# A list scheduler's rule for its filler work: the scalar engine's budget no longer gates it, and two groups of steps are placed elsewhere

## The chip, the cores and the metric

The kernel runs on one core of a Trainium2 chip. A core has a matrix engine (TensorE; PE in the profile, PEld for its weight loads), a vector engine (VectorE; DVE), a scalar engine (ScalarE; ACT), GpSimd (POOL) and a sync engine (SyncE; SP). In this kernel SP issues the weight loads and POOL issues the small reshuffling DMAs. Each engine works through its own instructions in order and waits at semaphores for the others. The metric is the device time of one execution in microseconds (us); less is better.

## The reference

The program computes two layers of an encoder trunk on 256 tokens of width 2048. Per layer, cut to what matters:

```python
h = rmsnorm(x, norm_g)
(c_a, c_glu, c_gate, q_down, kv_down, k_pe, m_gate, g_conv, g_mla) = split(h @ w_in)
# branch A
u = c_a * sigmoid(c_glu)
u = causal_depthwise_conv(u, conv_w, width=31) + conv_b
y_conv = (silu(layernorm(u)) * silu(c_gate)) @ w_proj_conv
# branch B: 16 heads, low-rank q and kv, rotary part of 64, block-causal mask in chunks of 64
q = rope(rmsnorm((rmsnorm(q_down) @ w_uq) per head))
k = rope(rmsnorm((rmsnorm(kv_down) @ w_ukv, k_pe) per head))
y_mla = (softmax(mask(q k^T * scale)) v * silu(m_gate)) @ w_proj_mla
# merge
x = x + (sigmoid(g_conv) * y_conv + sigmoid(g_mla) * y_mla) @ w_out
```

The rotary tables are sines and cosines of the positions times 32 inverse frequencies; they are computed once and serve both layers. The convolution is 31 taps per channel: a multiply-add over all tokens for each tap.

## The kernel before

**Products.** All matrix products run on TensorE in float32r. To keep float32 accuracy each operand is separated into a high and a low part, and a product takes three matmuls (high by high, high by low, low by high). The weights come from HBM in pieces of two 128-row blocks by up to 512 columns (`load`, five buffers, issued on SP). For each piece ScalarE makes the high part (`split_hi`, one cast) and VectorE the low part (`split_lo`, one subtraction). In the step of piece i the high part of piece i+3 and the low part of piece i+2 are issued (lines 181 and 281 to 285), and there are four and three buffers for them. So VectorE may lag behind TensorE's need by something under two steps before TensorE waits.

**Slots.** One piece is one slot: 12 matmuls on TensorE, then a call of `background(n)` (lines 242 to 260). A layer has 344 slots. `order_of_layer` gives the blocks: `glu` 0, `down` 0 to 2, `glu` 1 and 2, then eight rounds (one for each pair of heads) of `uq`, `ukv` and a further `glu` or `cgate` block, then the rest of `cgate`, `mgate`, `gmla`, `pmla`, `gconv`, `pconv` and `wout` blocks. `uq` and `ukv` blocks have two slots, all others eight.

**Two kinds of work beside the products.** Steps with a due slot are registered by `at_slot(ahead, f, vec, act)`. They run when their slot comes, and their stated costs are taken off a budget. The attention of a pair of heads is such a chain, placed by the constants of lines 67 and 68: squares and factors at 2 and 3 slots after the pair's `ukv` block, the turned queries and keys fetched at 7, transposed at 11, separated at 14 and 15 (with the subtractions a slot later), scores at 17, maxima at 18, exponentials at 19 with the probabilities written out by DMA, fetched back at 24, transposed at 29, values at 32.

The other kind has no due slot: `fill`, one queue in strict order. It holds the convolution (`conv`, 31 taps for each of 8 channel blocks of 256, queued when a block's input has been turned) and, queued by `layernorm` after the last pair, everything between the convolution and the `pconv` product: the mean (a matmul), subtracting it (`centre`, 8), the variance (a matmul), the reciprocal root in four pieces, scaling (`apply`, 8, each followed by a SiLU on ScalarE a slot later), the gate (`turned_gate` and `gated`, 8 each), and the separation of the result into high and low parts. A task may name a mark (`after`) and a number of slots that must have passed since.

**The budget.** At each slot both engines get the slot's length less the cost of the weight separation:

```python
slot = 12 * (n / 2400 + 0.0133) - 0.04
for e, split_us in (("vec", KS * n / 960 + 0.06), ("act", KS * n / 1066 + 0.04)):
    budget[e] = min(budget[e], 0.0) + slot - split_us
```

A debt is carried on; what is left over is lost. After the due steps, tasks are taken from `fill` while both budgets are above zero. For n = 512 that is 2.68 - 1.13 = 1.55 us for VectorE and 2.68 - 1.00 = 1.68 us for ScalarE.

**A tap** (lines 830 to 858) takes one of two forms. On VectorE alone it is two fused multiply-adds (cost 0.81). If ScalarE has scaled the input for it beforehand (`scale`, two activations, cost 0.85 of ScalarE), it is one addition on VectorE (cost 0.62). A tap orders the scaling of the next one where more than 0.8 is left in ScalarE's budget.

**At `pconv`** the product needs the whole normalised and gated convolution. The loop `while "yc" not in keep: run_fill()` and `before_pconv` take whatever is still in `fill` then, without looking at budgets, and TensorE's matmuls behind it wait for the result.

**Rotary tables.** `rope_tables` is a generator of 11 stages: two small loads (inverse frequencies, positions) on SP, nothing, the angles, six stages of range reduction on VectorE, and two stages with the sine activations. In layer 0, at `down` block 1, the stages are placed in slots 0 to 10 from the block's beginning. The same region has, counted from the start of the kernel, the loads of the layer's constants in slot 10 (`load_consts`, two DMAs on SP), the row factors `sum_x` in slot 13 (VectorE), and the evacuation of `glu` block 0 in slot 14. Slots 9 to 16 are `down` 0, 17 to 24 are `down` 1, 25 to 32 are `down` 2.

Of the kernel before, what the change touches and what calls it, by code (L numbers as in the profile page):

```python
# [63 lines left out]
EVAC_AT = 1  # L64
FETCH_AT, TURNED_AT = 4, 8

STATS_AT, SCALE_AT, QK_BACK_AT, QK_TURN_AT, ROPE_AT, NOPE_AT, SCORES_AT = 2, 3, 7, 11, 14, 15, 17
MAX_AT, EXP_AT, P_BACK_AT, P_TURN_AT, P_SPLIT_AT, VALUES_AT, O_AT = 18, 19, 24, 29, 30, 32, 34

REVOLUTION_PIECES = 6  # L70

# [44 lines left out]
def trunk(ctx: ExitStack, tc: tile.TileContext, xT, x, g_in, pos, win, wuq, wukv, wpc, wpm, wo, cst, rows, invf, out):  # L116
# [19 lines left out]
    pe, vec, act, gps, sp = (InOrder(e) for e in (nc.tensor, nc.vector, nc.scalar, nc.gpsimd, nc.sync))  # L136
# [83 lines left out]
    steps, clock, late = [], [0], []  # L220
    fill, budget, marks, owed = deque(), {"vec": 0.0, "act": 0.0}, {}, []

    def at_slot(ahead, f, vec=0.0, act=0.0):
        steps.append((clock[0] + ahead, (vec, act), f))

    def spend(costs):
        budget["vec"] -= costs[0]
        budget["act"] -= costs[1]
# [10 lines left out]
    def mark(name):  # L239
        marks[name] = clock[0]  # L240

    def background(n):
        clock[0] += 1
# [3 lines that stand above are left out]
        while True:  # L247
            due = [e for e in steps if e[0] <= clock[0]]
            if not due:
                break  # L250
            steps[:] = [e for e in steps if e[0] > clock[0]]
            for _, costs, f in due:
                spend(costs)
                f()
        while fill and budget["vec"] > 0 and budget["act"] > 0:
            after, slots = fill[0][1]
            if after and clock[0] < marks.get(after, 1 << 30) + slots:
                break
            run_fill()
        finish_late()  # L260

    def finish_late():
        while late:
            late.pop(0)()

    def run_fill():

        f, (after, _) = fill.popleft()
        while owed and after and after not in marks:
            owed.pop(0)()  # L270
        spend(f() or (0.0, 0.0))
# [29 lines left out]
    def stat_of(hi, lo):  # L301
        return lambda k, t: (hi[:, k, t * P : (t + 1) * P], lo[:, k, t * P : (t + 1) * P])
# [14 lines left out]
    def fetched(d, n):  # L317
        z = wide_p.tile([P, 4, n // P, 32], F32, tag="w", name="turned")
        fetch(d, z.rearrange("p i c s -> p (i c s)"))
        return z  # L320
# [152 lines left out]
    for l in range(DEPTH):  # L473
# [343 lines left out]
        def conv(b, us=us, vs=vs, s1=s1, C=C):  # L817
            scaled = {}

            def weight(k, j):  # L820
                at = C_CW + (2 * b + j) * CONV_W + k
                return C[:, at : at + 1]

            def scale(k):

                scaled[k] = wide_p.tile([P, 2, SEQ], F32, tag="w", name="tap")
                for j in range(2):
                    act.activation(scaled[k][:, j, :], us[b][:, j, k : k + SEQ], AF.Copy, scale=weight(k, j))

            def tap(k):  # L830

                if k == 0:
                    vs[b] = uv_p.tile([P, 2, PAD + SEQ], F32, tag="uv", name="v_t")
                u, v, costs = us[b], vs[b], (0.81, 0.0)
                if k == 0:
                    for j in range(2):
                        bias = C[:, C_CB + 2 * b + j : C_CB + 2 * b + j + 1]
                        vec.tensor_scalar(v[:, j, :SEQ], u[:, j, :SEQ], weight(k, j), bias, op0=ALU.mult, op1=ALU.add)
                elif k in scaled:
                    vec.tensor_add(v[:, :, :SEQ], v[:, :, :SEQ], scaled.pop(k))  # L840
                    costs = (0.62, 0.0)
                else:
                    for j in range(2):
                        vec.scalar_tensor_tensor(
                            v[:, j, :SEQ], u[:, j, k : k + SEQ], weight(k, j), v[:, j, :SEQ], op0=ALU.mult, op1=ALU.add
                        )
                if budget["act"] > 0.8 and 0 < k < CONV_W - 1:
                    scale(k + 1)
                    costs = (costs[0], 0.85)
                if k == CONV_W - 1:  # L850
                    mark(("s1", b))
                    if b == 0:
                        vec.tensor_copy(s1, v[:, :, :SEQ])
                    else:
                        vec.tensor_add(s1, s1, v[:, :, :SEQ])
                    costs = (costs[0] + 0.6, costs[1])
                    us.pop(b)
                return costs

            for k in range(CONV_W):  # L860
                fill.append((lambda k=k: tap(k), (None, 0)))

        def layernorm(vs=vs, s1=s1, C=C, keep=keep):
            stats = work2.tile([P, 5, SEQ], F32, tag="qk", name="ln_stats")
# [64 lines left out]
            def ahead(c):  # L929
                gates[c] = [fetched(d, 512) for d in keep["parked"][c]]  # L930
# [3 lines left out]
                return 0.65, 0.0  # L934

            def then(f, *args, after=None, slots=0):
                fill.append((lambda: f(*args), (after, slots)))

            fill.insert(max(len(fill) - 6, 0), (lambda: ahead(0), (None, 0)))
            for t in range(T):  # L940
                then(turned_gate, 0, t)
            then(mean, after=("s1", 7), slots=1)
# [174 lines left out]
        for kind, i, pl in planned:  # L1117
            if kind == "glu":
                at = EVAC_AT
                if i == 0 and l == 0:  # L1120
                    at = 6
                    for n, (t, c) in enumerate([(0, 0), (0, 2), (1, 0), (1, 2)]):
                        begin, end = first_sums(t, c)
                        at_slot((4, 5, 6, 9)[n], begin)
                        at_slot((9, 9, 10, 12)[n], end, 0.0, 1.5)
                    at_slot(13, sum_x, 2.2)
                elif i == 0:
                    at_slot(5, sum_x, 2.2)
                if i == 0:
                    at_slot(10, load_consts)  # L1130
                product(pl, uses_h, lambda t, ps, i=i: glu_evac(i, t, ps), at, (0.9, 2.2))
            elif kind == "down":
                if l == 0 and i == 1:
                    tables = rope_tables()
                    for a in range(11):
                        at_slot(a, lambda: next(tables, None), 0.0 if a < 2 else 1.6)
                product(pl, uses_h, lambda t, ps, i=i: down_evac(i, t, ps), costs=(0.0, 1.0))
                if i == len(DOWN_BLOCKS) - 1:
                    down_after()
            elif kind == "uq":  # L1140
                if i == 0:
                    attention_tiles()
                product(pl, of_down(0), lambda t, ps, i=i: uq_evac(i, t, ps), costs=(0.0, 2.3))
                at_slot(EVAC_AT + 1, lambda i=i: rotate_q(i), 1.2)
            elif kind == "ukv":
                product(pl, of_down(4), lambda t, ps, i=i: ukv_evac(i, t, ps), costs=(0.75, 2.6))
                attention(i)
                if i == NPAIR - 1:
                    layernorm()
            elif kind == "mgate":  # L1150
                product(pl, uses_h, lambda t, ps, i=i: mgate_evac(i, t, ps), costs=(1.25, 1.4))
            elif kind == "gmla":
                product(pl, uses_h, lambda t, ps, i=i: gmla_evac(i, t, ps), costs=(0.0, 2.7))
            elif kind == "pmla":
                product(pl, stat_of(*keep["o"]), lambda t, ps, i=i: pmla_evac(i, t, ps), costs=(1.25, 0.0))
            elif kind == "gconv":
                product(pl, uses_h, lambda t, ps, i=i: gconv_evac(i, t, ps), costs=(0.0, 3.9))
            elif kind == "cgate":
                product(pl, uses_h, lambda t, ps, i=i: cgate_evac(i, t, ps), costs=(0.0, 2.0))
            elif kind == "pconv":  # L1160
                while "yc" not in keep:
                    run_fill()
                product(pl, stat_of(*keep["yc"]), lambda t, ps, i=i: pconv_evac(i, t, ps), costs=(2.4, 0.0),
                        before=before_pconv if i == 0 else None)
            else:
                wout_begin(i)
                last = last_layer and i == 3
                product(pl, stat_of(*keep["y"]), lambda t, ps, i=i, f=wout_evac: f(i, t, ps),
                        0 if last else EVAC_AT, (1.25, 1.5))
# [103 lines left out]
```

## Time and profile before

| what | us |
|---|---|
| median of 3 runs | 1962.25 |
| lowest and highest of them | 1960.39, 1964.64 |
| the profiled execution, its own time | 1963.85 |
| its span, first to last instruction | 1961.9 |
| TensorE busy in the span | 1912.8 |
| VectorE busy | 1598.0 |
| ScalarE busy | 1350.8 |
| GpSimd busy | 371.1 |

The profile is of one execution. A page gives the busy time of each engine, the busy share in 40 equal slices of the span, the costliest groups of instructions and the DMA issues. Further views list the waits (who waited for whom), the instructions in order of time, and the busy time of each engine in chosen stretches. A line of code there is that of a helper through which every instruction is issued (L127), so instructions are told apart by the names of their tiles: `lo<-raw,hi` is the low part of a weight piece, `hi<-raw` the high part, `tap<-u_t,cst` the scaling of a tap, `v_t<-v_t,tap` a tap's addition, `v_t<-u_t,cst,v_t` half of a tap on VectorE alone, `acc` a product's accumulator, `ycT` the separated operand of `pconv`, `s` the scores, `qk_t` their operands.

### The profile page before, as it was taken

To read this page: it belongs to the slowest core of one execution; us is meant where nothing else is said; L and a number is where in the kernel's file an instruction comes from. 1 tells how busy PE (TensorE), PEld (TensorE's weight loads), DVE (VectorE), ACT (ScalarE), POOL (GpSimd) and SP (SyncE) were. 2 spreads that over 40 slices of the span, in tenths; PEclk is the share of its full clock that TensorE was granted. 3 is DMA by queue.
4 is the path that set the end of the run, shared out by engine and by line. 5 is a ranking of instruction groups with operands and counts; after the bars stand their busy time and mean duration, and the time that the engine had idled before them with its cause. 6 is when DMAs were issued, how large, how long until landed. Compare 5 with 4: busy or idle time off the path is not lost. (4 is left out here: it accounts for less than half of the span.)

```text
span 1961.9 us, 27462 instructions
## 1 busy us (share of the span) xinstructions
PE 1912.8 (97%) x8787; PEld 1607.8 (82%) x8787; DVE 1598.0 (81%) x2592; ACT 1350.8 (69%) x2385; POOL 371.1 (19%) x694
## 2 busy tenths in 40 slices
PE   9999999999999999699999999999999999997999
PEld 8888888888888887488889888888888888885887
DVE  6888887889999998566669788878899999985654
ACT  6577878878787885444557678688778878764442
POOL 1023434332200000021210333343322000001200
PEclk9999999999999999799999999999999999998999
DMA  8657877777755556277866687777767655664764
GB/s 307 204 198 255 269 241 253 257 247 231 239 195 199 187 205 214 86 236 242 292 216 201 210 261 246 238 249 258 246 229 240 201 196 185 210 210 137 246 226 162
DMA packets 135569, 437.73 MB, mean 223 GB/s; under 512 B 22784, under 2 KB 26624, under 8 KB 135424
## 3 DMA queue, kind: packets, MB, share of 16 engines
q1 hardware_dynamic: 104688, 359.63, 54.4%
q0 software_dynamic: 30304, 76.06, 12.6%
q8 instruction: 69, 1.13, 0.2%
q14 instruction: 76, 0.62, 0.1%
q10 hardware_dynamic: 432, 0.28, 0.0%
HBM read 395.51 MB, written 40.37 MB: 222 GB/s over the span
## 5 line engine op out<-in xcount | busy, mean ns | idle before, releaser
L127 ACT CAST hi<-raw 128x1024 fp32r<-128x1024 f32 (+3 forms) x689 | 703.4, 1024 | 525.1 <-PE acc L127 441.3
L127 DVE TENSOR_TENSOR lo<-raw,hi 128x1024 fp32r<-128x1024 f32 (+3 forms) x689 | 811.9, 1183 | 247.5 <-PE acc L127 180.3
L127 PE MATMUL acc<-hi,hT 128*128 128x512 f32 (+2 forms) x1728 | 525.9, 383 | 0.0
L127 PEld LDWEIGHTS acc<-hi,hT 128*128 128x128 f32 x1728 | 322.7, 188 | 59.6
L127 PE MATMUL acc<-lo,h_hi 128*128 128x512 f32 (+2 forms) x864 | 331.1, 383 | 2.8 <-DVE lo L127 2.8
L127 PE MATMUL acc<-hi,h_hi 128*128 128x512 f32 (+2 forms) x864 | 331.3, 383 | 0.7 <-ACT hi L127 0.7
L127 PE MATMUL acc<-lo,hT 128*128 128x512 f32 (+2 forms) x864 | 330.7, 383 | 0.1
L127 PE MATMUL acc<-hi,h_lo 128*128 128x512 f32 (+2 forms) x864 | 330.2, 382 | 0.0
L127 ACT ACTIVATE tap<-u_t,cst 128x256 f32<-128x256 f32 x634 | 274.9, 499 | 0.0
L127 DVE TENSOR_TENSOR v_t<-v_t,tap 128x512 f32<-128x512 f32 x317 | 218.4, 689 | 21.2 <-ACT tap L127 4.7
L127 PE MATMUL acc<-hi,ycT 128*128 128x512 f32 x512 | 171.1, 415 | 31.7 <-ACT ycT L127 31.7
L127 PEld LDWEIGHTS acc<-lo,h_hi 128*128 128x128 f32 x864 | 162.2, 188 | 34.9 <-DVE lo L127 5.5
L127 PEld LDWEIGHTS acc<-hi,h_hi 128*128 128x128 f32 x864 | 162.4, 188 | 30.6 <-ACT hi L127 1.2
L127 PEld LDWEIGHTS acc<-lo,hT 128*128 128x128 f32 x864 | 162.5, 188 | 30.4 <-DVE lo L127 0.8
L127 PEld LDWEIGHTS acc<-hi,h_lo 128*128 128x128 f32 x864 | 162.2, 188 | 30.1
L127 POOL DMA_DIRECT2D turned<-turn_d x82 | 46.0, 561 | 596.9 <-DVE v_t L127 191.7
L127 PE MATMUL acc<-hi,yT 128*128 128x512 f32 x512 | 158.5, 389 | 0.0
L127 PE MATMUL acc<-hi,oT 128*128 128x512 f32 x512 | 157.9, 389 | 0.0
L127 POOL DMA_DIRECT2D turn_d<-gate x176 | 95.9, 552 | 301.9 <-DVE gate L127 253.1
L127 PEld LDWEIGHTS acc<-hi,ycT 128*128 128x128 f32 x512 | 103.5, 202 | 58.0 <-ACT ycT L127 34.7
L127 PE MATMUL acc<-hi,qkc 128*128 128x512 f32 (+1 forms) x512 | 146.9, 362 | 0.0
L127 DVE SCALAR_TENSOR_TENSOR v_t<-u_t,cst,v_t 128x256 f32<-128x256 f32 x326 | 140.9, 479 | 1.4
(165 smaller groups left out, 2259.3 us busy)
## 6 DMA issues: line engine op xcount, KB each, us to landing
raw<-in_win SPq DMA_DIRECT2D x383, 512.0 KB, 4.3
raw<-in_wpm SPq DMA_DIRECT2D x64, 512.0 KB, 3.3
raw<-in_wpc SPq DMA_DIRECT2D x64, 512.0 KB, 4.0
raw<-in_wo SPq DMA_DIRECT2D x64, 512.0 KB, 4.4
raw<-in_wukv SPq DMA_DIRECT2D x32, 512.0 KB, 4.0
turned<-turn_d POOLq DMA_DIRECT2D x50, 256.0 KB, 4.4
raw<-in_win SPq DMA_DIRECT2D x32, 384.0 KB, 4.3
raw<-in_wuq SPq DMA_DIRECT2D x32, 384.0 KB, 3.1
```

Of the source, the lines that this page charges most:

```text
L127: ins = getattr(self.engine, name)(*a, **k)
```

## The change

Three parts. The loop over `fill` looks at VectorE's budget alone; ScalarE's counts only for tasks that say so in a third entry, and `apply` is the one that does (it must not be negative then). Scores, maxima, exponentials and the fetch of the probabilities stand one slot later; what follows them stays. The rotary tables start at `down` block 0, two slots after its beginning, in place of the beginning of block 1, and their stated cost is 1.8 in place of 1.6.

```diff
-STATS_AT, SCALE_AT, QK_BACK_AT, QK_TURN_AT, ROPE_AT, NOPE_AT, SCORES_AT = 2, 3, 7, 11, 14, 15, 17
-MAX_AT, EXP_AT, P_BACK_AT, P_TURN_AT, P_SPLIT_AT, VALUES_AT, O_AT = 18, 19, 24, 29, 30, 32, 34
+STATS_AT, SCALE_AT, QK_BACK_AT, QK_TURN_AT, ROPE_AT, NOPE_AT, SCORES_AT = 2, 3, 7, 11, 14, 15, 18
+MAX_AT, EXP_AT, P_BACK_AT, P_TURN_AT, P_SPLIT_AT, VALUES_AT, O_AT = 19, 20, 25, 29, 30, 32, 34
...
-        while fill and budget["vec"] > 0 and budget["act"] > 0:
-            after, slots = fill[0][1]
-            if after and clock[0] < marks.get(after, 1 << 30) + slots:
+        while fill and budget["vec"] > 0:
+            after, slots, scalar = fill[0][1]
+            if after and clock[0] < marks.get(after, 1 << 30) + slots or scalar and budget["act"] < 0:
                 break
             run_fill()
...
-        f, (after, _) = fill.popleft()
+        f, (after, _, _) = fill.popleft()
...
-                fill.append((lambda k=k: tap(k), (None, 0)))
+                fill.append((lambda k=k: tap(k), (None, 0, False)))
...
-                fill.append((lambda: f(*args), (after, slots)))
-
-            fill.insert(max(len(fill) - 6, 0), (lambda: ahead(0), (None, 0)))
+                fill.append((lambda: f(*args), (after, slots, f is apply)))
+
+            fill.insert(max(len(fill) - 6, 0), (lambda: ahead(0), (None, 0, False)))
...
-                if l == 0 and i == 1:
+                if l == 0 and i == 0:
                     tables = rope_tables()
                     for a in range(11):
-                        at_slot(a, lambda: next(tables, None), 0.0 if a < 2 else 1.6)
+                        at_slot(a + 2, lambda: next(tables, None), 0.0 if a < 2 else 1.8)
```

## The prediction

> **What bounds the kernel now.** First the page: busy time by engine, and two rows of the 40 slices.
>
> ```profile
> PE 1912.8 (97%) x8787; PEld 1607.8 (82%) x8787; DVE 1598.0 (81%) x2592; ACT 1350.8 (69%) x2385; POOL 371.1 (19%) x694
> ...
> PE   9999999999999999699999999999999999997999
> ...
> PEclk9999999999999999799999999999999999998999
> ```
>
> TensorE is the bound except in two places: slice 17, where its busy share and its clock both drop, and slice 37. The waits of TensorE say what is late there:
>
> ```profile
> PE acc L127 <- ACT ycT L127: 31.7, 7, 5.6
> PE s L127 <- DVE qk_t L127: 6.8, 18, 1.9
> PE acc L127 <- DVE lo L127: 2.8, 7, 0.7
> ```
>
> (Total, times, longest, in us.) `ycT` is `pconv`'s operand: the convolution branch is not ready. What it costs shows in stretches: length, then busy time and count of PE, PEld, DVE, ACT, POOL, then the granted clock and the DMAs.
>
> ```profile
> 475.00:700.00 225.00, 225.00 (x1001) 186.52 (x1000) 216.97 (x302) 178.80 (x298) 16.46 (x30) 1.00 0.61 206
> 760.00:788.00 28.00, 22.86 (x101) 18.59 (x99) 23.34 (x36) 17.90 (x25) 2.19 (x4) 0.95 0.61 202
> 788.00:835.00 47.00, 31.97 (x96) 24.39 (x97) 23.02 (x35) 19.19 (x27) 0.00 (x0) 0.74 0.26 88
> 1764.00:1805.00 41.00, 29.44 (x98) 22.49 (x98) 21.78 (x32) 17.92 (x24) 0.00 (x0) 0.79 0.34 116
> ```
>
> Undisturbed, 1001 matmuls leave in 225 us (a few merely straddle an edge): 0.226 us each, so a slot of 12 is 2.72 us. `pconv` block 0 has 96 matmuls and so needs 21.8 us. In layer 0 the stretches of 28 and 47 us hold 197 matmuls, 44.5 us of work, and lose 30.5; in layer 1 41 us hold 98, 22.1 us, and lose 18.9. Together 49.4: the 31.7 of waiting, and 17.7 in which the granted clock is 0.74 to 0.95 behind the waits.
>
> By a rule of the Trainium skill ("TensorE: Matmul & The Clock Gate", Part 1) the array falls to half clock after an idle window of about 3.4 us and needs one busy window to come back; estimated from that page, seven stalls would add at most 7 x 1.7 = 12 us and both stalls would be worth 44. The granted clock agrees in kind; the trace's 17.7 us is more, and it decides.
>
> **Part 1: the filler without ScalarE's gate.** Is VectorE's time there to be had? Taking the loop slot by slot with the code's own costs, in layer 0 before `pconv` 53 slots end with VectorE budget left because ScalarE's is used up, 31.9 us lost in all (layer 1: 53 and 33.2); `fill` comes to `pconv` with 18 tasks in layer 0 and 11 in layer 1. The same count gives 317 assisted taps and 163 on VectorE alone, which is what the trace has:
>
> ```profile
> L127 DVE TENSOR_TENSOR v_t<-v_t,tap 128x512 f32<-128x512 f32 x317 | 218.4, 689 | 21.2 <-ACT tap L127 4.7 <-DVE v_t L127 0.5
> L127 DVE SCALAR_TENSOR_TENSOR v_t<-u_t,cst,v_t 128x256 f32<-128x256 f32 x326 | 140.9, 479 | 1.4
> L127 ACT ACTIVATE tap<-u_t,cst 128x256 f32<-128x256 f32 x634 | 274.9, 499 | 0.0
> ```
>
> (326 halves are 163 taps.) With the new condition the count gives 264 assisted and 216 alone: ScalarE sheds 53 x 2 x 0.499 = 53 us, VectorE is charged 53 x (0.81 - 0.62) = 10 us more, 5 per layer. Of layer 0's 31.9 us, 27 remain, 27 / 1.55 = 17 slots: the mean's matmul goes from slot 267 to slot 250. `fill` is then empty in slot 274, `pconv` begins in slot 281; in layer 1 it is empty nine slots ahead. The loop at `pconv` finds nothing to run. That removes the stall whole, waits and clock: **-49.4 us**.
>
> Does VectorE carry a budget that is used up in every slot? The durations say no: 1.2 us for a low part and 0.96 for a tap alone exceed the stated 1.13 and 0.81. But a duration is not what an instruction takes from its successor:
>
> ```profile
> 600.31 1.22 DVE L127 TENSOR_TENSOR lo<-raw,hi 128x1024 fp32r<-128x1024 f32 x1
> ...
> 601.45 0.88 DVE L127 SCALAR_TENSOR_TENSOR v_t<-u_t,cst,v_t 128x256 f32<-128x256 f32 x2
> ...
> 602.24 1.22 DVE L127 TENSOR_TENSOR lo<-raw,hi 128x1024 fp32r<-128x1024 f32 x1
> ...
> 603.38 1.49 DVE L127 TENSOR_TENSOR v_t<-v_t,tap 128x512 f32<-128x512 f32 x2
> 604.90 0.69 DVE L127 TENSOR_TENSOR s1c<-s1c,v_t 128x512 f32<-128x512 f32 x1
> 605.51 1.22 DVE L127 TENSOR_TENSOR lo<-raw,hi 128x1024 fp32r<-128x1024 f32 x1
> ```
>
> From start to start the low part takes 1.14, a tap alone 0.79, an addition 0.61 where the next instruction does not need it and 0.75 where it does. The stated costs are right on average. And some blocks are already filled to the last slot by this count, `gmla` 1 and `pmla` 1 of layer 0 among them:
>
> ```profile
> 541.50:563.30 21.80, 21.80 (x98) 18.03 (x97) 21.14 (x30) 18.25 (x29) 0.00 (x0) 1.00 0.50 172
> 628.60:650.30 21.70, 21.70 (x97) 17.99 (x96) 20.82 (x29) 18.25 (x33) 0.00 (x0) 1.00 0.56 191
> ```
>
> VectorE is busy 97% there and TensorE never waits. So a full budget is just carried; the matmuls are its cover. In the attention stretch TensorE's slots are longer than planned (scores and values are not in `slot`):
>
> ```profile
> 238.30:264.10 25.80, 25.45 (x125) 21.30 (x124) 22.86 (x54) 18.97 (x41) 6.75 (x13) 1.00 0.71 228
> 1214.50:1244.30 29.80, 27.60 (x125) 22.51 (x124) 25.64 (x55) 19.75 (x42) 8.57 (x16) 0.94 0.68 225
> ```
>
> 25.8 us for 8 slots, against 21.4 planned: there is more room. A full queue leaves less slack behind VectorE's own waits, though. Bounds: 0, and 1 us for each of the 16 pairs, 16 us; I take **+1**, near the saturated blocks, which show none.
>
> ScalarE's gate stays for `apply`: it costs waiting in at most 8 slots per layer by the count, inside the margin of 7 and 9 slots. If that margin were gone, each missing slot would cost 2.72 us.
>
> **Part 2: scores a slot later.** The subtractions that make the scores' operands are issued in slot 16 after the pair, the scores stood in 17; a VectorE that lags more than a slot makes TensorE wait there, with all further matmuls behind it. The two rows above are the same block with the same 125 matmuls: the second has the longest of these waits (1.9) and the clock at 0.94, and is 4.0 us longer; so 2 us of clock come on top of the 6.8 of waits. A slot later the operands have to be ready no later than the low part that TensorE needs next anyway. Bounds -3 (the large waits alone) and -9; I take **-7**. On VectorE the maxima follow in the next slot as before. POOL issues the fetch of the probabilities a slot later, four slots ahead of the transposition:
>
> ```profile
> L127 POOL DMA_DIRECT2D pr<-turn_d x16: 567/567/570, 202.6 to 1427.6; - x16
> L127 DVE STREAM_TRANSPOSE pr<-pr x16: 944/948/951, 218.4 to 1448.4; 128x768 f32<-128x768 f32 x16
> ...
> DMA to landing us min/median/max: 2.4/3.4/5.5
> ```
>
> Issued at 202.6, used at 218.4: 15.8 us for 5.5 at most; one slot less costs nothing. The four write-out DMAs per pair now stand behind, not ahead of, the next pair's fetch on POOL's queue (both were in slot 19), which can only help that fetch.
>
> **Part 3: the rotary tables.** They move from slots 17 to 26 to slots 10 to 20, six slots, not eight. What they cost now, against the same blocks in layer 1:
>
> ```profile
> 47.40:65.30 17.90, 17.48 (x99) 16.60 (x97) 12.68 (x44) 7.31 (x10) 3.22 (x7) 1.00 0.57 179
> 65.30:81.70 16.40, 14.81 (x97) 14.02 (x96) 13.28 (x37) 8.87 (x15) 0.00 (x0) 1.00 0.62 203
> 1027.60:1044.30 16.70, 16.70 (x99) 16.70 (x98) 15.51 (x27) 12.99 (x24) 0.00 (x0) 1.00 0.57 174
> 1044.30:1058.30 14.00, 14.00 (x97) 14.00 (x96) 13.58 (x24) 12.87 (x24) 0.00 (x0) 1.00 0.71 220
> ```
>
> 34.3 against 30.7: 3.6 us lost. The new place is worse. Its two loads go out in slot 10, right behind the constants on SP, and `sum_x` falls among the stages:
>
> ```profile
> 34.78 0.42 SPq L127 DMA_DIRECT2D down<-in_rows  x1
> ...
> 37.53 0.96 DVE L127 TENSOR_TENSOR lo<-raw,hi 128x768 fp32r<-128x768 f32 x1 [1.14 <-ACT hi L127]
> 39.18 0.96 DVE L127 TENSOR_TENSOR lo<-raw,hi 128x768 fp32r<-128x768 f32 x1 [0.69 <-PE acc L127]
> 40.05 0.15 DVE L127 TENSOR_REDUCE totx<-ss_x 128x2 f32<-128x8 f32 x1
> ...
> 42.53 0.96 DVE L127 TENSOR_TENSOR lo<-raw,hi 128x768 fp32r<-128x768 f32 x1
> ...
> 59.63 0.95 DVE L127 TENSOR_TENSOR lo<-raw,hi 128x768 fp32r<-128x768 f32 x1
> ...
> 62.20 0.95 DVE L127 TENSOR_TENSOR lo<-raw,hi 128x768 fp32r<-128x768 f32 x1
> ...
> down<-in_rows SPq DMA_DIRECT2D x1, 576.0 KB, 7.2
> ...
> pos_t<-in_pos SPq DMA_DIRECT2D x1, 1.0 KB, 3.3
> ```
>
> The constants' rows land at 34.8 + 7.2 = 42.0; taking landings in the order of issue, the positions come at 42.2, while VectorE, in slot 12, stands there from 38.4 (37.53 plus 0.87): 3.8 us of waiting with its low parts queued behind. Then `sum_x` takes 42.53 - 40.05 = 2.5, and a slot with a stage 62.20 - 59.63 = 2.57 against TensorE's 16.7 / 8 = 2.09. Angles done at 43.3; low part of slot 13 at 44.2; `sum_x`, a stage and the next low part, 49.2; a stage, the product of `glu` 0 (0.8) and a low part, 52.5; then 2.57 each: 55.1, 57.7, 60.2, 62.8. TensorE needs these for slots 15 to 21 from 43.3 on, every 2.09: slot 21 would start at 55.8 and starts at 62.8. That is 7.0 lost in place of 3.6: **+3.4**. Bounds: -3.6 (all of it covered) and +6.
>
> The Trainium skill ("DMA: Bandwidth & Descriptors", Queues, rings and completion order) states that completion is not first-in first-out per issuing engine. By that rule the small load could land 3.3 us after its own issue, at about 39.9; the wait would be 1.5, and this part would come to +1.1. Here, at 50 us, the landings did follow the issues.
>
> **The sum.** -49.4 + 1 - 7 + 3.4 = -52 from the profiled execution's 1963.85 gives 1911.9. That execution was 1.6 above the median, so **1910**.
>
> **The rivals.**
> *VectorE becomes the bound (slower).* If the durations counted, a full slot would need 1.22 + 1.55 x 1.14 = 2.99 of VectorE (1.14: the mean of 0.96 / 0.81 and 0.69 / 0.62) against 2.72. Outside the attention stretch some 280 slots would be full: +76, less the 53: about 1985. It decides from 0.19 us per slot on. For it: 97% busy leaves little. Against: the start-to-start times and the two blocks above. 7%.
> *Slack is eaten in the attention stretch.* VectorE's waits for turned data hit the low parts: the 16 us bound, 1925. 12%.
> *The stall only shrinks.* The chain mean, centre, variance, root, apply, gate has waits of its own; if half of the stall stays, 1935. Against: 17 slots gained for an overhang of 18 tasks. 8%.
> *The change does not do what it says:* ScalarE's gate was not what held the queue. Against: the 53 slots, and a count of taps that fits exactly. About 1960, 3%.
>
> **How the numbers follow.** My forecast, with parts 2 and 3 anywhere in their bounds (1902 to 1916), has 70%. The range 1901 to 1926 takes in the second rival and leaves the others out. A difference under 0.2% (4 us) cannot be told from none: faster 0.90 (forecast, 12%, 8%), same 0.03, slower 0.07.
>
> **What would show it.** Right: no wait of `acc` for `ycT` and a clock of 1.00 through `pconv` 0; 264 `v_t<-v_t,tap` and 528 `tap`; mean matmuls some 45 us earlier; no wait of `s` for `qk_t`; a wait of `posf` for `pos_t` near 38 us and low parts late until about 63. Wrong: waits of `acc` for `lo` spread from 80 to 740 us, or `pconv` 0 still longer than 22 us.

## The result, and the profile after

The changed kernel takes 1918.35 us (median of 4 runs, 1918.15 to 1918.5), beside 1963.45 for the kernel before on the same chip: a ratio of 0.9769, interval 0.9751 to 0.9788. That is 45 us less, where the prediction had 52; the 7 between are mainly two larger errors of opposite sign, as the runs below show.

The page of the changed kernel: TensorE and VectorE busy, and the slices for TensorE and its clock.

```profile
PE 1897.0 (99%) x8787; PEld 1592.6 (83%) x8787; DVE 1601.6 (84%) x2645; ACT 1305.7 (68%) x2280; POOL 371.5 (19%) x694
...
PE   8999999999999999999999999999999999999999
...
PEclk9999999999999999999999999999999999999999
```

Both dents (slices 17 and 37) are gone. Busy time alone would mislead: TensorE's falls by only 16 us, since matmuls at a low clock are busy for longer, and since a recorded matmul lasts longer than its turn (see "The scores"), so that part of a wait counts as busy. What TensorE waits for now (total us, times, longest):

```profile
PE acc L127 <- DVE lo L127: 11.3, 27, 2.5
PE acc L127 <- DVE su L127: 2.1, 2, 1.0
```

`ycT` and `qk_t` have left the list; low parts (`lo`) have moved up from 2.8, and `su`, the evacuation of a `glu` block, is new. The groups that count the taps (count, then busy us, mean ns, idle before):

```profile
L127 ACT ACTIVATE tap<-u_t,cst 128x256 f32<-128x256 f32 x528 | 229.5, 499 | 3.1 <-DVE v_t L127 2.5
...
L127 DVE SCALAR_TENSOR_TENSOR v_t<-u_t,cst,v_t 128x256 f32<-128x256 f32 x432 | 186.5, 479 | 0.8
...
L127 DVE TENSOR_TENSOR v_t<-v_t,tap 128x512 f32<-128x512 f32 x264 | 182.2, 690 | 19.6 <-ACT tap L127 2.1
```

264 assisted taps and 216 (432 halves) on VectorE alone, which is the count of the prediction. Five stretches, in the columns of the prediction: the first two cover `down` 0 and `down` 1, the third `pmla` 0 to 3 of layer 0, the last two `pconv` 0 of each layer.

```profile
30.80:52.20 21.40, 18.27 (x97) 17.64 (x96) 12.87 (x42) 13.65 (x27) 0.72 (x2) 0.94 0.63 211
52.20:71.20 19.00, 18.23 (x98) 16.83 (x98) 16.18 (x52) 9.08 (x15) 5.08 (x10) 0.97 0.67 188
...
608.20:699.20 91.00, 89.47 (x386) 71.23 (x384) 87.31 (x128) 68.89 (x118) 1.09 (x2) 1.00 0.58 191
789.40:811.10 21.70, 21.70 (x97) 17.99 (x96) 9.80 (x8) 9.61 (x10) 0.00 (x0) 1.00 0.63 193
1737.40:1759.20 21.80, 21.80 (x98) 18.02 (x97) 9.80 (x8) 9.61 (x10) 0.00 (x0) 1.00 0.60 193
```

`pconv` 0 now takes its undisturbed 21.8 us at a clock of 1.00. In the `pmla` stretch 91.0 us hold only 386 matmuls, where 0.226 us each would make 87.2: TensorE is late there, at full clock, with VectorE busy 96%.

Every matmul start in the trace gives the length of each block, from its first matmul to the next block's. Grouped (us, both layers together except the first row), for the two kernels and eight of the experiments that follow:

| blocks | before | after | e1 | e2 | e3 | e4 | e7 | e9 | e10 | e11 |
|---|---|---|---|---|---|---|---|---|---|---|
| `down` 0 to 2, layer 0 | 51.0 | 54.5 | 50.5 | 50.7 | 55.0 | 54.7 | 47.4 | 47.4 | 47.4 | 47.4 |
| attention: `uq` 0 to `cgate` 2 | 562.4 | 551.8 | 565.8 | 548.5 | 562.6 | 551.7 | 551.7 | 551.3 | 557.7 | 567.3 |
| `gmla` 0 to `gconv` 2 | 481.3 | 493.7 | 492.5 | 479.3 | 482.0 | 482.3 | 482.3 | 482.2 | 482.2 | 482.2 |
| `gconv` 3 and `pconv` 0 | 137.6 | 87.0 | 87.0 | 179.4 | 129.9 | 87.0 | 87.0 | 95.6 | 98.3 | 98.5 |

All other blocks together differ from before by under 2.5 us. In the third and fourth rows 0.9 us of the difference from before is no gain or loss: the statistics matmuls of layer 0 moved from one to the other.

### The profile page after: what moved, and what is told of

Same layout as the page of the kernel before. It is cut to its first block, busy times and chain, and to the rows that moved or that the text cites. A ratio compares the mean times of both kernels' runs of the same rounds, so it can differ in the third digit from the quotient of the medians.

```text
span 1916.6 us, 27420 instructions
## 1 busy us (share of the span) xinstructions
PE 1897.0 (99%) x8787; PEld 1592.6 (83%) x8787; DVE 1601.6 (84%) x2645; ACT 1305.7 (68%) x2280; POOL 371.5 (19%) x694
## 4 chain that ended last, share of the span: by engine, by line
PE 80%; DVE 13%; issue 5%; ACT 1%; DMA 1%; SPq 0%; DVEq 0%; POOL 0%; ACTq 0%
PE acc L127 77%; DVE lo L127 5%; DVE v_t L127 4%; PE s L127 1%; PE o_ps L127 1%; DVE qk L127 1%; DVE tables L127 0%; DVE qk_t L127 0%; DVE ym L127 0%; ACT hi L127 0%; ACT tap L127 0%; DMA pos_t<-in_pos 0%; DMA raw<-in_win 0%; DVE rsq_t L127 0%; SPq L127 0%
## 5 line engine op out<-in xcount | busy, mean ns | idle before, releaser
L127 ACT ACTIVATE tap<-u_t,cst 128x256 f32<-128x256 f32 x528 | 229.5, 499 | 3.1 <-DVE v_t L127 2.5
L127 DVE TENSOR_TENSOR v_t<-v_t,tap 128x512 f32<-128x512 f32 x264 | 182.2, 690 | 19.6 <-ACT tap L127 2.1
L127 DVE SCALAR_TENSOR_TENSOR v_t<-u_t,cst,v_t 128x256 f32<-128x256 f32 x432 | 186.5, 479 | 0.8
L127 PE MATMUL acc<-hi,ycT 128*128 128x512 f32 x512 | 157.8, 389 | 0.0
L127 POOL DMA_DIRECT2D turn_d<-su x128 | 69.7, 552 | 225.9 <-DVE su L127 225.9
```

The lines of the kernel that those rows point to most:

```text
L127: ins = getattr(self.engine, name)(*a, **k)
```

## The experiments

### The three parts alone

**e1_taps** is the kernel before with part 1 only (the third entry of the tasks included).

```diff
-        while fill and budget["vec"] > 0 and budget["act"] > 0:
+        while fill and budget["vec"] > 0:
...
-            if after and clock[0] < marks.get(after, 1 << 30) + slots:
+            if after and clock[0] < marks.get(after, 1 << 30) + slots or scalar and budget["act"] < 0:
```

> The kernel before with part 1 alone: the filler looks at VectorE's budget only; scores and tables stand where they stood. Theory (the trace of after): the stall at pconv goes whole, -50 us, and a VectorE that is full in every slot gives back about 19 us of it as waits for low parts, so about 1932 (1926 to 1938). Rival (the sizes of my prediction): -49 + 1, about 1915.

1929.25 us, ratio 0.9825 (0.981 to 0.984): inside the theory's range, and not the rival's. TensorE's waits:

```profile
PE s L127 <- DVE qk_t L127: 9.6, 22, 1.9
PE acc L127 <- DVE lo L127: 7.7, 18, 1.0
```

The wait for `ycT` is gone with part 1 alone, and `gconv` 3 with `pconv` 0 is already at 87.0. The price stands beside it: 11.2 us more in `gmla` 0 to `gconv` 2 (0.9 of it the moved statistics), and 3.4 in the attention blocks, where the scores now wait 9.6 in place of 6.8 and their 16 batches take 2.6 us more.

**e2_scores** is the kernel before with part 2 only.

```diff
-STATS_AT, SCALE_AT, QK_BACK_AT, QK_TURN_AT, ROPE_AT, NOPE_AT, SCORES_AT = 2, 3, 7, 11, 14, 15, 17
+STATS_AT, SCALE_AT, QK_BACK_AT, QK_TURN_AT, ROPE_AT, NOPE_AT, SCORES_AT = 2, 3, 7, 11, 14, 15, 18
-MAX_AT, EXP_AT, P_BACK_AT, P_TURN_AT, P_SPLIT_AT, VALUES_AT, O_AT = 18, 19, 24, 29, 30, 32, 34
+MAX_AT, EXP_AT, P_BACK_AT, P_TURN_AT, P_SPLIT_AT, VALUES_AT, O_AT = 19, 20, 25, 29, 30, 32, 34
```

> The kernel before with part 2 alone: scores, maxima, exponentials and the fetch one slot later. Theory (the trace of after, where the 16 batches of scores take 1.89 us each, before 1.89 to 5.30): -15 to -17 us, about 1947. Rival (my prediction's -7, the waits that the profile names): about 1956. The stall at pconv stays in both.

1989.1 us, ratio 1.0128 (1.0113 to 1.0144): slower than before by 26 us, which neither the theory nor the rival had. Its waits, and its additions of taps:

```profile
PE acc L127 <- ACT ycT L127: 56.0, 8, 14.6
PE var L127 <- DVE ln_stats L127: 10.9, 2, 9.4
```

```profile
L127 DVE TENSOR_TENSOR v_t<-v_t,tap 128x512 f32<-128x512 f32 x331 | 228.3, 690 | 24.0 <-ACT tap L127 6.1 <-DVE v_t L127 0.9
```

The scores do what they should: the wait for `qk_t` is gone, and the attention blocks take 13.9 us less. But the stall at `pconv` grew from 31.7 to 56.0 us, with a new one at the variance. The slot-by-slot count of the prediction, run on this kernel, gives 331 assisted taps, as the row does, and says why: with the scores and exponentials a slot later, 69 and 74 slots (layer 0, layer 1) end on ScalarE's budget in place of 53 and 53, VectorE loses 46.8 and 48.3 us of budget in place of 31.9 and 33.2, and `fill` reaches `pconv` with 35 and 29 tasks in place of 18 and 11. Part 2 under the old rule starves the filler. It is worth having only behind part 1.

**e3_tables** is the kernel before with part 3 only.

```diff
-                if l == 0 and i == 1:
+                if l == 0 and i == 0:
...
-                        at_slot(a, lambda: next(tables, None), 0.0 if a < 2 else 1.6)
+                        at_slot(a + 2, lambda: next(tables, None), 0.0 if a < 2 else 1.8)
```

> The kernel before with part 3 alone: the rotary tables from slot 10. Theory, and my prediction: +3.4 us, about 1967, with VectorE waiting 3.7 us for the positions at about 38 us. Rival (the move hides the tables): -3.6, about 1960.

1960.71 us (10 runs), ratio 0.9986 (0.9977 to 0.9995). The total is the rival's, but not for its reason. The mechanism of the theory is there: `down` 0 to 2 take 55.0 in place of 51.0, and `lo` waits of up to 2.5 appear.

```profile
PE acc L127 <- ACT ycT L127: 26.6, 7, 5.6
...
PE acc L127 <- DVE lo L127: 5.9, 8, 2.5
```

But budgets in other slots change too. By the count 14 tasks instead of 18 are left at `pconv` of layer 0 (314 assisted taps, as the trace has). The wait for `ycT` falls by 5.1, and the `pconv` row of the table by 7.7. As in e2, a part tried alone acts through the stall, which part 1 removes.

### Where VectorE's full budget costs

**e4_split** is the changed kernel with each addition of a tap issued as two halves: the same arithmetic, but no instruction needs the result of the one just ahead of it.

```diff
-                    vec.tensor_add(v[:, :, :SEQ], v[:, :, :SEQ], scaled.pop(k))
+                    scaled_k = scaled.pop(k)
+                    for j in range(2):
+                        vec.tensor_add(v[:, j, :SEQ], v[:, j, :SEQ], scaled_k[:, j, :])
```

> The changed kernel with each assisted tap's addition issued as two additions of 256 columns, so that neighbouring instructions on VectorE no longer depend on each other. Theory: the full slots overrun because an addition whose neighbour needs its result takes 0.73 to 0.81 us from start to start and not 0.62; two halves take about 0.67 whatever stands beside them, the overrun of 0.11 us per slot goes, and 8 to 12 us of the waits for low parts with it: 1907 to 1911. Rival (VectorE is full because of the amount of work): 264 instructions more make it slower, 1919 to 1925.

1906.79 us, ratio 0.9711 (0.9695 to 0.9727), 0.2 us below the theory's range: the theory holds. `gmla` 0 to `gconv` 2 falls from 493.7 to 482.3, and a stretch of the same 91 us over `pmla` of layer 0 in this kernel holds 403 matmuls in 91 us, where the changed kernel had 386:

```profile
600.00:691.00 91.00, 91.00 (x403) 75.34 (x402) 90.81 (x179) 73.59 (x129) 1.09 (x2) 1.00 0.61 197
```

VectorE's timelines show the mechanism (start us, duration, instruction, count). The changed kernel, in `pmla` 1:

```profile
640.75 1.22 DVE L127 TENSOR_TENSOR lo<-raw,hi 128x1024 fp32r<-128x1024 f32 x1
641.89 2.28 DVE L127 TENSOR_TENSOR v_t<-v_t,tap 128x512 f32<-128x512 f32 x3
644.09 1.22 DVE L127 TENSOR_TENSOR lo<-raw,hi 128x1024 fp32r<-128x1024 f32 x1
645.22 0.88 DVE L127 SCALAR_TENSOR_TENSOR v_t<-u_t,cst,v_t 128x256 f32<-128x256 f32 x2
646.21 0.69 DVE L127 TENSOR_TENSOR v_t<-v_t,tap 128x512 f32<-128x512 f32 x1
646.81 1.22 DVE L127 TENSOR_TENSOR lo<-raw,hi 128x1024 fp32r<-128x1024 f32 x1
```

And e4_split:

```profile
634.33 0.87 DVE L127 SCALAR_TENSOR_TENSOR v_t<-u_t,cst,v_t 128x256 f32<-128x256 f32 x2
635.12 0.75 DVE L127 TENSOR_TENSOR v_t<-v_t,tap 128x256 f32<-128x256 f32 x2
635.79 1.21 DVE L127 TENSOR_TENSOR lo<-raw,hi 128x1024 fp32r<-128x1024 f32 x1
636.93 2.09 DVE L127 TENSOR_TENSOR v_t<-v_t,tap 128x256 f32<-128x256 f32 x6
638.94 1.21 DVE L127 TENSOR_TENSOR lo<-raw,hi 128x1024 fp32r<-128x1024 f32 x1
```

Three additions take 644.09 - 641.89 = 2.20 whole and 638.94 - 636.93 = 2.01 in halves. A tap on VectorE alone with an addition behind it takes 646.81 - 645.22 = 1.59 whole and 635.79 - 634.33 = 1.46 in halves. Stated are 3 x 0.62 = 1.86 and 0.81 + 0.62 = 1.43. So what such a slot does costs 0.16 to 0.34 more than stated in the changed kernel and 0.03 to 0.15 more in e4_split.

**e8_true_cost** leaves the additions whole and corrects what the list scheduler believes of them.

```diff
-                    costs = (0.62, 0.0)
+                    costs = (0.72, 0.0)
```

> The changed kernel with nothing but the stated cost of an assisted tap's addition raised from 0.62 to 0.72, nearer to the 0.75 that the trace shows as its mean from start to start. By the slot count the mean moves from slots 250 and 590 to 258 and 598, and two tasks are left at pconv of layer 0. Theory (full slots are overbooked by their stated cost): most waits for low parts from gmla to gconv 0 go, at most 3 us return at pconv: 1908 to 1912. Rival (VectorE is full because of the amount of work, whatever the plan says): the waits stay, 1917 to 1921.

1906.33 us, ratio 0.9706 (0.9689 to 0.9722), a little better than the theory's range. (Its expectation gives 0.75 as an addition's mean; the trace has 0.69, or 0.73 as worked out below.) The blocks of the third row come to 482.2, as in e4_split, by fewer taps in a slot rather than cheaper ones (285 assisted, 195 alone), and `pconv` 0 is still undisturbed. A true price and a lower price cure the same wait: what was wrong was the stated cost.

### The tables

**e5_tables_back** is the changed kernel without part 3.

```diff
-                if l == 0 and i == 0:
+                if l == 0 and i == 1:
...
-                        at_slot(a + 2, lambda: next(tables, None), 0.0 if a < 2 else 1.8)
+                        at_slot(a, lambda: next(tables, None), 0.0 if a < 2 else 1.6)
```

> The changed kernel with part 3 taken back: the tables start at down block 1 again. Theory (with the filler free of ScalarE's budget the tables' place matters only by what it costs at down 0 to 2): 3.4 us less than the changed kernel, about 1915. Rival (the earlier tables let the filler start earlier, as they did when moved alone): more than the changed kernel, about 1921.

1912.67 us, ratio 0.9737 (0.9722 to 0.9752). Part 3 costs 5.7 us inside the changed kernel, where the theory had 3.4: 3.5 in the `down` blocks (51.0 to 54.5), as in the prediction's mechanism, and most of the rest in `gmla` 0 to `gconv` 2 (491.0 here, 493.7 in the changed kernel); the cause of the latter was not followed further.

**e6_loads_early** is the changed kernel with the two loads one slot sooner, ahead of the constants on SP.

```diff
-                        at_slot(a + 2, lambda: next(tables, None), 0.0 if a < 2 else 1.8)
+                        at_slot(a + 2 if a else 1, lambda: next(tables, None), 0.0 if a < 2 else 1.8)
```

> The changed kernel with the tables' two small loads issued one slot earlier, ahead of the constants' loads on SP; all stages stay. Theory: the positions land before VectorE asks for them, its wait of 3.7 us goes and TensorE gets it back whole, because the slack behind VectorE is used up there: about 1914.6. Rival (the wait lies in slack, or the earlier stages run into the next thing): within 1 us of 1918.4.

1914.92 us, ratio 0.9749 (0.9734 to 0.9763), as the theory had it. VectorE in the changed kernel (in brackets: idle time before the instruction, and what ended it), then in e6_loads_early:

```profile
37.56 0.96 DVE L127 TENSOR_TENSOR lo<-raw,hi 128x768 fp32r<-128x768 f32 x1 [1.15 <-ACT hi L127]
42.23 0.17 DVE L127 CAST posf<-pos_t 128x2 f32<-128x2 int32 x1 [3.71 <-DMA pos_t<-in_pos]
```

```profile
37.68 0.96 DVE L127 TENSOR_TENSOR lo<-raw,hi 128x768 fp32r<-128x768 f32 x1 [1.14 <-ACT hi L127]
38.56 0.17 DVE L127 CAST posf<-pos_t 128x2 f32<-128x2 int32 x1
```

The 3.71 us of waiting are gone, but the time falls by 3.4, and the stages still stand one to a slot: `down` 0 to 2 is still 50.7 in place of 47.4.

**e7_split_spread** joins e4's halves with early loads and the stages in every second slot.

```diff
-                        at_slot(a + 2, lambda: next(tables, None), 0.0 if a < 2 else 1.8)
+                        at_slot(2 * a + 6 if a > 1 else 1, lambda: next(tables, None), 0.0 if a < 2 else 1.8)
```

> The split additions together with tables that are spread: loads in slot 9, the nine computing stages in every second slot from 18 to 34. A stage then takes 1.71 us out of two slots that leave 1.0 to 1.2 us each. Theory: the 7 us that down 0 to 2 lose in the changed kernel go, and 1906.8 becomes about 1900. Rival (the later stages push the filler back and the stall at pconv returns in part): 1905 or more.

**1899.7 us**, ratio 0.9673 (0.9659 to 0.9687): the theory's number and the best version of all, 18.7 us under the changed kernel. `down` 0 to 2 takes the undisturbed 47.4, which is what these blocks take in layer 1 of the kernel before. TensorE is left with `lo` waits of 3.3 us and the `su` waits:

```profile
PE acc L127 <- DVE lo L127: 3.3, 8, 0.8
PE acc L127 <- DVE su L127: 2.1, 2, 1.0
```

**e9_cost_spread** has e8's cost and e7's tables, with whole additions.

```diff
-                    costs = (0.62, 0.0)
+                    costs = (0.72, 0.0)
...
-                        at_slot(a + 2, lambda: next(tables, None), 0.0 if a < 2 else 1.8)
+                        at_slot(2 * a + 6 if a > 1 else 1, lambda: next(tables, None), 0.0 if a < 2 else 1.8)
```

> The changed kernel with the addition's stated cost at 0.72 and the tables spread (loads in slot 9, stages in every second slot from 18 to 34); additions are whole. Theory: 1906.3 less the 7 us of down 0 to 2, about 1899.5, level with the split additions. Rival: two tasks more at pconv, 1903 or more.

1909.3 us, ratio 0.9726 (0.9711 to 0.974): the theory falls, and the rival had it. The two cures don't add, since both take VectorE time from the filler. By the count 10 tasks are left at `pconv` of layer 0 (2 in e8, none in e7), and the old stall is back in small:

```profile
PE acc L127 <- ACT ycT L127: 6.2, 2, 3.3
PE acc L127 <- DVE lo L127: 2.3, 5, 0.8
```

`gconv` 3 and `pconv` 0 take 95.6 in place of 87.0. Halves need no such margin, which is why e7 wins.

### The scores

**e11_no_part2** is e9 without part 2.

```diff
-STATS_AT, SCALE_AT, QK_BACK_AT, QK_TURN_AT, ROPE_AT, NOPE_AT, SCORES_AT = 2, 3, 7, 11, 14, 15, 18
+STATS_AT, SCALE_AT, QK_BACK_AT, QK_TURN_AT, ROPE_AT, NOPE_AT, SCORES_AT = 2, 3, 7, 11, 14, 15, 17
-MAX_AT, EXP_AT, P_BACK_AT, P_TURN_AT, P_SPLIT_AT, VALUES_AT, O_AT = 19, 20, 25, 29, 30, 32, 34
+MAX_AT, EXP_AT, P_BACK_AT, P_TURN_AT, P_SPLIT_AT, VALUES_AT, O_AT = 18, 19, 24, 29, 30, 32, 34
```

> The kernel of e9 with the scores, maxima, exponentials and fetch back in their slots of before. Theory (part 2 alone is worth what the 16 batches of scores lost, about 15 us, once the filler no longer depends on ScalarE's budget; less the 5 us of waits that it brings): 10 to 13 us more than e9, about 1911. Rival (my prediction's -7): 1906. Rival (its effect on the filler, +42 when moved alone, has a counterpart here): outside 1900 to 1916.

1925.09 us, ratio 0.9803 (0.9787 to 0.982): part 2 is worth 15.8 us there, more than the theory or the first rival had. The time lies in the range of the second rival, but the filler is not the reason: by the count 10 tasks and none are left at the two `pconv`, as in e9, and the waits for `ycT` are the same 6.2 us. Between the two profiled executions, 19.5 us apart in span, the attention blocks account for 16.0 (567.3 against 551.3). Another 2.9 stand at `gconv` 3 and `pconv` 0: behind the same two waits the clock is halved for 10.2 us in e11 and for 3.4 in e9, so this part is no effect of part 2 that the runs show. The wait of the scores is back:

```profile
PE s L127 <- DVE qk_t L127: 9.5, 18, 1.9
```

9.5 us of waits for 16 us of time: the 16 batches of scores take 18.4 us more than in e9, and the two `uq` 2 blocks 2.4 less. One such place shows where the rest is: TensorE at a pair's scores in the kernel before (the wait in brackets), then in the changed kernel.

```profile
251.90 0.71 PE L127 MATMUL s<-qk_t 128*128 128x256 f32 x2
252.82 1.93 PE L127 MATMUL s<-qk_t 128*128 128x256 f32 x14 [0.21 <-DVE qk_t L127]
254.59 0.40 PE L127 MATMUL acc<-hi,h_hi 128*128 128x512 f32 x1
```

```profile
223.43 2.05 PE L127 MATMUL s<-qk_t 128*128 128x256 f32 x16
225.32 0.40 PE L127 MATMUL acc<-hi,h_hi 128*128 128x512 f32 x1
```

From the first score to the next product it is 254.59 - 251.90 = 2.69 before and 225.32 - 223.43 = 1.89 after: 0.80 lost where the view of waits shows 0.21. A wait is counted from the recorded end of the instruction ahead, and a recorded matmul lasts longer than its turn: 16 of them follow each other every 1.89 / 16 = 0.12 us. Over the 16 batches the kernel before spends 15.3 us more than 16 x 1.89 (1.89 twice, mostly 2.67 to 2.69, once 5.30); the changed kernel takes 1.89 in each.

**e10_exp_late** is e9 with the exponentials and the fetch behind them one more slot later, against the new `su` waits.

```diff
-MAX_AT, EXP_AT, P_BACK_AT, P_TURN_AT, P_SPLIT_AT, VALUES_AT, O_AT = 19, 20, 25, 29, 30, 32, 34
+MAX_AT, EXP_AT, P_BACK_AT, P_TURN_AT, P_SPLIT_AT, VALUES_AT, O_AT = 19, 21, 26, 29, 30, 32, 34
```

> The last kernel with the exponentials and the fetch another slot later (21 and 26; maxima stay at 19). In the changed kernel the exponentials with their table load stand right ahead of the sigmoid of the next glu block on ScalarE, VectorE waits up to 3.6 us for that sigmoid, and low parts and the accumulator come late once per pair. Theory: with the sigmoid first these waits (2.1 us of acc for su, 3 us of acc for lo in the attention stretch) go: about 1895. Rival (something else waits instead: the probabilities, 9 us ahead of their use in the changed kernel, come too late, or ScalarE's casts do): 1899 or more.

1917.48 us, ratio 0.9768 (0.9753 to 0.9782): the theory is wrong, and 8 us are lost against e9. The cause of the `su` waits had been read on ScalarE in the changed kernel:

```profile
194.01 1.28 ACT L127 ACT_TABLE_LOAD   x1
195.31 0.49 ACT L127 ACTIVATE pr<-sx,nb,rs_p 128x128 f32<-128x128 f32 x1
...
197.36 1.04 ACT L127 CAST hi<-raw 128x1024 fp32r<-128x1024 f32 x1
198.42 1.28 ACT L127 ACT_TABLE_LOAD   x1
199.72 0.84 ACT L127 ACTIVATE su<-acc,rinv_x 128x256 f32<-128x256 f32 x2
```

and on its VectorE, which stands behind that sigmoid:

```profile
200.22 0.88 DVE L127 SCALAR_TENSOR_TENSOR su<-acc,rinv_x,su 128x256 f32<-128x256 f32 x2 [3.51 <-ACT su L127]
```

A table load, the exponentials, a cast and a second table load lie ahead of the sigmoid; VectorE is idle for 3.51 us and its next low part is late. In e10 the exponentials are behind the sigmoid, and the `su` wait is gone, but now the casts (`hi`) come late behind them, as the rival had it (VectorE's waits for them are 34.2 us in place of 15.2 in e9):

```profile
PE acc L127 <- DVE lo L127: 9.1, 12, 1.0
...
DVE lo L127 <- ACT hi L127: 34.2, 21, 2.7
```

The attention blocks take 557.7 in place of 551.3. (The 2.7 more at `pconv` are, as in e11, a longer time at the low clock behind the same two waits.) The same work of ScalarE stands ahead of one thing that VectorE waits for or of another. Not tried: charging the scores and values as slot length in the budget, and other orders within a slot.

## Why the prediction was right, and where not

**The three parts in sequence.** Before to e1 is part 1, e1 to e5 adds part 2, e5 to the changed kernel adds part 3. (e1 and e5 ran on different chips, on which the kernel before takes 1963.40 and 1963.56.)

| part | predicted | measured (medians) |
|---|---|---|
| 1, the filler | -49.4 + 1 = -48.4 | 1929.25 - 1963.4 = -34.1 |
| 2, the scores | -7 | 1912.67 - 1929.25 = -16.6 |
| 3, the tables | +3.4 | 1918.35 - 1912.67 = +5.7 |
| sum | -52 | -45.0 |

**The stall: right to the term.** Predicted -49.4. Block by block, `gconv` 3 and `pconv` 0 go from 137.6 to 87.0, less the 0.9 moved: -49.7. Count of taps, empty `fill` at `pconv` and a granted clock of 1.00 are as predicted; the mean's matmul of layer 0 comes 39.5 us earlier (706.0 in place of 745.5), where some 45 were expected. In e2_scores the count gave a longer stall and more assisted taps, and both came, so the reading that ScalarE's gate held the queue stands on runs in both directions.

The Trainium skill ("TensorE: Matmul & The Clock Gate", Part 1) lets the clock recover after at least one busy window of about 3.4 us; by the prediction's estimate from it, with one window for each stall, the stalls were worth 44. The measured 49.7 is more. Narrow stretches of the kernel before, in the columns of the prediction, show why:

```profile
785.00:791.80 6.80, 3.71 (x9) 2.89 (x10) 3.27 (x6) 6.11 (x10) 1.09 (x2) 0.50 0.47 155
791.80:798.60 6.80, 3.78 (x17) 2.76 (x15) 4.38 (x7) 4.01 (x5) 0.00 (x0) 1.00 0.35 120
798.60:805.40 6.80, 4.79 (x11) 3.76 (x12) 1.91 (x4) 2.48 (x5) 0.00 (x0) 0.50 0.09 36
```

The granted clock is either 0.50 or 1.00 here; the 0.74 to 0.95 of the wider stretches are mixtures. Each of the seven stalls has one stretch at 0.50, six of 6.8 us and one of 3.4, 44.4 us in all, and between them the clock is back at 1.00. TensorE is busy in 34.0 of the 44.4 us, and at half the clock half of that is lost: 17.0, against the 17.7 that the prediction read from the wider stretches. So the estimate was short in one term: it gave each stall one window of 3.4 us, and six of the seven took two.

**Carrying a full VectorE budget: the step that failed in size.** "The stated costs are right on average", and with it the +1 that was taken. Measured: 493.7 - 481.3 - 0.9 = 11.5 us in `gmla` 0 to `gconv` 2, plus 0.2 ahead of them, inside the bound of 16 but far from the value taken. The view of waits shows only 4.3 us of it, 2.6 in layer 0 and 1.7 in layer 1; waits for `lo` on the way to `pconv` are what the prediction had named as a sign of being wrong. Two readings went wrong. The prediction had 0.75 for an addition whose result is needed next and 0.61 otherwise, and took the mean to be the stated 0.62; in layer 0 of the changed kernel the mean from start to start is 0.69 (0.70 in the kernel before), and 0.73 with what the fused instructions ahead of additions lose (27 times 0.19, spread over some 130 additions). And it argued from two blocks that were full without stalling. Between such blocks stood the 53 slots that ended with VectorE budget left, and they kept up a slack between the end of a low part and the first matmul of its piece: a mean of 2.9 to 3.8 us in the `pmla` blocks of layer 0. With every slot full from `mgate` on it is used up; in the changed kernel the mean is about zero there (1.7 to 2.2 in e4_split, 3.7 to 4.1 in e8_true_cost). The rival "slack is eaten" has the mechanism, but put it in the attention stretch; it came mostly in the blocks ahead of `pconv`. With part 1 alone the attention stretch loses 3.4 us, not 16, 2.6 of it at the scores; part 2 takes this back. e4_split and e8_true_cost, which change the two sides of that cost, remove it alike.

**The scores: right in direction, mis-sized.** The bounds were -3 and -9, and -7 was taken, from 6.8 of waits and 2 of clock. Measured -16.6 behind part 1 and 15.8 in e9 against e11, new `su` waits included. The waits view was taken as the whole loss, and it shows 6.8 of the 15.3 us that the batches of the kernel before lose. The `su` waits were not foreseen. The prediction looked only at VectorE, where "the maxima follow in the next slot as before", and did not follow where ScalarE's exponentials would come to stand, which is ahead of a sigmoid. These waits lengthen the `uq` 2 block by 1.2 us in each layer.

**The tables: right.** +3.4 predicted; 54.5 - 51.0 = +3.5 in the blocks where it was put, with the wait of `posf` (3.71, predicted 3.8) in its place. Its effect in the whole kernel is 5.7, within the bound of 6. SP issues the loads in this order in the changed kernel:

```profile
34.80 0.42 SPq L127 DMA_DIRECT2D down<-in_rows  x1
...
35.74 0.71 SPq L127 DMA_DIRECT2D pos_t<-in_pos  x1
```

and the 1 KB of positions are used at 42.23, as the landing in order of issue had it. In e6, issued ahead of the constants, they are there in time for 38.56.

The Trainium skill ("DMA: Bandwidth & Descriptors", Queues, rings and completion order) states that completion is not first-in first-out; by that rule about 39.9 was possible. It forbids no order, but the landing seen here is the one in order of issue.

**The other rivals.** VectorE did not become the bound (1985). Its mechanism has begun, though: the rival decides from 0.19 us per slot on, and a slot of `pmla` 0 to 3 in layer 0 ran over by (91.0 - 87.2) / 32 = 0.12. The stall did not merely shrink (1935). That the sum came out near is luck: the errors by part are +14.3 (in e1_taps the full budget costs 10.3 and the attention blocks 3.4, where +1 was taken), -9.6 for the scores and +2.3 for the tables, and they cancel for the most part.

## What to carry to other kernels

A list scheduler's stated cost of a short vector instruction must be its start-to-start time in the order in which it will run; raising the load to the limit turns an error of 0.1 us in each instruction into a wait in each slot. Where a wait of TensorE is to be priced, measure from the first matmul behind the waiting place to the next product and set it against an undisturbed batch, instead of adding up the waits view. And parts of a change that share a budget are not additive: part 2 alone made this kernel 26 us slower and, behind part 1, 16 us faster.

## What the runs showed of the hardware

- **Dependent neighbours on VectorE.** In layer 0 of the changed kernel a 512-element addition takes 0.61 us from start to start with an unrelated instruction next (66 cases), 0.79 with an addition into the same tile next (49) and 0.73 with a fused multiply-add on it (14). A 256-element fused multiply-add takes 0.40 ahead of one on the other half and 0.58 ahead of an addition over both (27). In halves (e4_split) an addition takes 0.34 for each half whatever follows, 0.68 for both: dearer than 0.61, cheaper than 0.73 or 0.79, and the fused multiply-add ahead of it takes 0.41. So 0.12 to 0.19 us is paid for needing the result of the instruction just ahead, and alternating two halves hides it.
- **Clock behind stalls.** Removing the 31.7 us of waits for `ycT` gave 49.7 us. Behind or during each of the seven waits the granted clock was 0.50, for 3.4 us with the one wait of 2.1 us and for 6.8 us with the six of 4.4 to 5.6, and matmuls followed each other every 0.427 us in place of 0.227. The price of a wait varies: the same two waits, 6.2 us together, had 3.4 us at 0.50 in e9_cost_spread and 10.2 us in e11_no_part2.
- **A table switch on ScalarE** costs 1.28 us each way here: a batch of exponentials between two sigmoids pays it twice, and VectorE, behind that sigmoid, waited 3.51 us in the place shown.
